# Mixer of a decoder layer: small TensorE steps at counted distances, narrow inverse and state products

## The chip, the cores and the metric

The kernel runs on one core of a Trainium2 chip. The metric is device time in microseconds, the median of several executions. TensorE is PE in the profile, VectorE is DVE, ScalarE is ACT, GpSimd is POOL, and SyncE, which issues most loads, is SP.

## The reference, cut to what matters

One layer of a hybrid decoder, for 256 prompt tokens and one token each of 8 sample sequences. D is 2048, the hidden width 5632, all in float32:

```python
x = x + 0.5 * swiglu(rms_norm(x, g1), w1, w3, w2)          # ffn1
x = x + mixer_block(rms_norm(x, gm), ...)
x = x + mem_attend(rms_norm(x, gq), mem_k, mem_v, w_q, w_o)
x = x + 0.5 * swiglu(rms_norm(x, g2), w1, w3, w2)          # ffn2

# mixer_block
proj = h @ w_in                          # qkv (conv), z, b, a, q_s, k_s, v_s, two gates
# gated delta rule, 8 heads of 128, chunks (the reference takes 64, the kernel 128):
lmat = eye + beta * (k @ k.T) * decay    # lower triangular, unit diagonal
u_v, w_k = solve(lmat, [beta * v, beta * gamma * k])
u = u_v - w_k @ S;  o = q_g @ S + (q @ k.T * decay) @ u;  S = g_end * S + k_end.T @ u
o_g = rms_norm(o) * silu(z)
# sliding window attention, 16 query heads on 4 key heads of 64, window 128, with a sink:
o_s = softmax_with_sink(mask(q_s @ k_s.T / 8)) @ v_s
out = (sigmoid(gate_gdn) * (o_g @ w_br_gdn) + sigmoid(gate_swa) * (o_s @ w_br_swa)) @ w_out
```

The sample rows do one step of the same rule on 8 stored states per head (128x128 each) and attend to a stored cache of 128 keys.

## The kernel before

The activations are kept transposed: 16 chunks of 128 features by 264 columns (256 prompt, 8 sample). Every weight product runs in fp32r with both operands split in a high and a low part. `gemm` (L169) loads a block of weights `raw` (128x1024, L153, from SP's queue, four buffers), ACT casts it to `wh` (L154, three buffers), DVE subtracts to `wl` (L155, four buffers), and PE does three products for each 128x128 tile: `wh` by `xh` (L184), `wh` by `xl` (L185), `wl` by `xh` (L186). A block of four chunks and two column tiles is 24 products of 128x264. These "big products" fill most of every stage: ffn1, the mixer, the memory attention, ffn2.

The mixer's other work is small. `gemm_ba` (L343) makes the decay and beta scalars, with three transposes at L361 to L363. For each of four head pairs `conv_pair` (L435) projects and convolves q, k, v and z, `gdn_pair` (L462) does the prompt's chunked rule for four arrays at once (two heads by two chunks), and `gdn_sample` the eight sample states. The triangular inverse in `gdn_pair` doubles its block size level by level: L536 transposes the first level, then five levels follow, each with four products A by U (L545, 64 columns, into `pP`), a mask on DVE (L547), four products with T (L550, into `pU`), a subtraction on DVE (L551), and transposes of U (L555) with a copy to T on ACT (L556); L560 to L566 close it. The outputs come at L570 to L594, the square, mean and scaling of the output norm at L599 to L609, and its transposes at L612. In `gdn_sample` each of 16 states per pair is the stationary operand of a product with two columns (L653); the states are loaded by SP at the start of that function. Sliding window attention has a projection with rope, then `swa_prompt` for each of four key groups: scores (L770), mask and maximum on DVE (L773 to L779), exponentials on ACT (L780, L782), sum and reciprocal on DVE (L783, L784), scaling on ACT (L786), transposes (L791), a copy (L792), products with the values (L797). One group has three such blocks. `swa_sample` does the same for the sample rows.

In the source the steps stand one after the other, "c0 c1 s c2 w0 c3 w1 x w2 w3", and then 12 of 16 gate products. The order in which each engine really runs them is chosen at build time by a scheduler with a simulated timeline, which takes whichever instruction it expects to be ready: the small steps of one pair end up between big products of later steps. Only in the memory attention are PE's instructions kept in source order (`pin`). PSUM tiles `gd` and `sw` (two buffers each) hold results of small products.

Of the kernel before, what the change touches and what calls it, by code (L numbers as in the profile page):

```python
# [30 lines left out]
    0, 128, 256, 384, 512, 640, 960, 1224, 1488)  # L31
C_N = 1744


def constants():
# [9 lines left out]
    c[:, C_M1:C_M1 + P] = (i % 2 == 1) & (j == i - 1)  # L45
    for n in range(5):
        s = 2 << n
        q = np.arange(64)
        col = (q // s) * 2 * s + s + q % s
        blk = (i // (2 * s) == col[None, :] // (2 * s)) & (i % (2 * s) < s)  # L50
        c[:, C_LV + n * 64:C_LV + (n + 1) * 64] = blk
# [4 lines left out]
    c[:, C_SN:C_SN + TOK] = np.sin(ang) * np.where(np.arange(P) % 64 < 32, -1.0, 1.0)[:, None]  # L56
    k = np.arange(2 * P)[None, :]
# [12 lines left out]
class Build:  # L70
    def __init__(self, ctx, tc, i, o, phases):
        self.tc, self.nc, self.i, self.o = tc, tc.nc, i, o
        nc = self.nc
# [95 lines left out]
    def gemm(self, W, n0, nw, xs, evac, k0=0, steps=()):  # L169
# [18 lines left out]
        for j in range(nt):  # L188
            evac(j, ps[j][:, :TOK])

# [77 lines left out]
    def mixer(self, norm, nxt):  # L268
# [9 lines left out]
        if True:  # L278
            with self.phase("mc") as mc, self.phase("gd", 2, PSUM) as gd, self.phase("sw", 2, PSUM) as sw:
# [21 lines left out]
            for n, g in gates[12:14]:  # L301
                self.gate(win, xs, n, g)
            sp = {"og": self.split_in("og", self.og), "os": self.split_in("os", self.os)}
            for n, g in gates[14:]:
# [38 lines left out]
    def gemm_ba(self, win, xs):  # L343
        nc, mc = self.nc, self.mc
        idn = self.K(C_ID)
        bt = mc.tile([P, 3, 16], F32, name="bt")

# [6 lines left out]
        for c in range(NCH):  # L354
            for k in range(2):
                nc.tensor.matmul(acc, HL[:, c], xs[c][k], start=(c == 0 and k == 0), stop=(c == NCH - 1 and k == 1))
        ba = self.gp.tile([P, TOK], F32, name="cy", bufs=2)[0:32]
        nc.vector.tensor_tensor(out=ba, in0=acc, in1=self.norm.finish()[0:32], op=ALU.mult)
        pt = self.evt()
        i32 = idn[0:32, 0:32]  # L360
        nc.tensor.transpose(pt[:, 0:32], ba[:, 0:P], i32)  # L361
        nc.tensor.transpose(pt[:, 32:64], ba[:, P:NP], i32)
        nc.tensor.transpose(pt[0:NS, 64:96], ba[:, NP:TOK], i32)  # L363
# [22 lines left out]
        nc.vector.scalar_tensor_tensor(out=g, in0=a, scalar=-1.0, in1=b3(ea), op0=ALU.mult, op1=ALU.mult)  # L386
        pg = self.evt()
        nc.tensor.matmul(pg[:, 0:16], self.K(C_UI), g[:, 0:2, :], start=True, stop=True)
        nc.tensor.matmul(pg[:, 16:32], self.ones, g[:, 0:2, :], start=True, stop=True)
# [15 lines left out]
        nc.vector.tensor_tensor(out=dg[:, 1], in0=bc(gs, NS), in1=i8, op=ALU.mult)  # L405
        pb = self.evt()
        nc.tensor.matmul(pb[:, 0:128], self.ones[0:NS, :], dg.rearrange("p a h b -> p (a h b)"), start=True, stop=True)
# [27 lines left out]
    def conv_pair(self, win, xs, p):  # L435
        nc, mc = self.nc, self.mc
        pt = lambda name: mc.tile([P, 2, TOK], F32, name=name, bufs=2)
        self.kp, self.qp, self.vp, self.zp = pt("kp"), pt("qp"), pt("vp"), pt("zp")
        self.conv_group(win, xs, 8 + 2 * p, self.kp)
        self.conv_group(win, xs, 2 * p, self.qp)  # L440
        self.conv_group(win, xs, 16 + 2 * p, self.vp)
        zp = self.zp
# [8 lines left out]
        self.gemm(win, OFF_Z + 2 * p * P, 256, xs, ev)  # L451

# [9 lines left out]
    def gdn_pair(self, p):  # L462
        nc, mc, o = self.nc, self.mc, self.o
        idn = self.K(C_ID)
# [4 lines left out]
        qT = [self.qp[:, hl(a), sl(a)] for a in A4]  # L469
        kT = [self.kp[:, hl(a), sl(a)] for a in A4]  # L470
        vT = [self.vp[:, hl(a), sl(a)] for a in A4]
# [8 lines left out]
        for a in A4:  # L480
            nc.tensor.transpose(pq[:, a], qT[a], idn)
        sq = self.gt("sq")
        nc.scalar.activation(out=sq, in_=pq, func=AF.Square)
        nc.vector.tensor_reduce(out=ss[:, 4:8], in_=sq, axis=AX.X, op=ALU.add)
        pk = self.ps4()
        for a in A4:
            nc.tensor.transpose(pk[:, a], kT[a], idn)
        sq = self.gt("sq")
        nc.scalar.activation(out=sq, in_=pk, func=AF.Square)
        nc.vector.tensor_reduce(out=ss[:, 0:4], in_=sq, axis=AX.X, op=ALU.add)  # L490
        nc.vector.tensor_scalar(out=ss, in0=ss, scalar1=4 * EPS, scalar2=None, op0=ALU.add)
# [7 lines left out]
        ke = self.gt("ke")  # L499
        TT(out=ke, in0=pk, in1=bc(gE, P), op=ALU.mult)  # L500
        kb = self.gt("kb", 2)
        TT(out=kb, in0=pk[:, 1::2], in1=bc(skb[:, 1::2], P), op=ALU.mult)
        pv = self.ps4()
        for a in A4:
# [772 lines left out]
```

## Time and profile before

| | us |
|---|---|
| Median of three runs | 2515.12 (2513.25 to 2518.91) |
| Profiled execution, own time | 2517.21 |
| Its span, first to last instruction | 2515.4 |
| The mixer up to the last small step of its heads | 782 to 1416 of that span |

A timeline row tells when an instruction (or a run of the same ones, "x4") begins and how long it is shown as busy. PE overlaps its instructions, so the rows of two products overlap, and what a product costs is the distance from its start to the next one's. A float32 product has two rows, a float32 transpose and an fp32r product one. "Idle before" tells how long an engine stood still ahead of an instruction, and the name behind the arrow what ended that.

### The profile page before, as it was taken

The page shows a single profiled execution, that of the slowest core. Times are in us where ns is not written, and L with a number is a line of the kernel's source. Part 1 is how long each engine was busy: PE and PEld are TensorE (multiplying, and loading weights), DVE is VectorE, ACT ScalarE, POOL GpSimd, SP SyncE. Part 2 cuts the span into 40 slices and gives each one's busy share as a digit, 9 for nine tenths or more (in the row PEclk, how much of TensorE's full clock was granted, in tenths as well). Part 3 has the DMA queues.
Part 4 walks back from the last instruction along what each step waited for, and adds up shares of the span by engine and source line. Part 5 has one row for each costly group of instructions (what it writes and reads, how often), then busy time and mean ns, then how long its engine had stood idle before and what let it go on. Part 6 is the DMA issues. An engine that isn't in the chain of part 4 may idle for free. (4 is left out here: it accounts for less than half of the span.)

```text
span 2515.4 us, 48048 instructions
## 1 busy us (share of the span) xinstructions
PE 2469.8 (98%) x19960; PEld 2434.6 (97%) x19960; DVE 1508.7 (60%) x2495; ACT 1102.5 (44%) x1631; POOL 109.2 (4%) x159
## 2 busy tenths in 40 slices
PE   7999999999999999999999999999999999999997
PEld 7999999999999998998999999979999999999997
DVE  6555544555556867776575677678555545555554
ACT  5444333444444543454454445445444333444443
POOL 0000000000000002010120410000000000000000
PEclk9999999999999998999999999999999999999999
DMA  6656566656666556454555876765655566565554
GB/s 205 183 178 183 174 181 184 181 180 181 179 178 192 160 154 207 149 160 140 162 160 161 261 220 211 221 235 154 183 182 178 176 183 185 178 183 178 177 172 131
DMA packets 136091, 455.22 MB, mean 181 GB/s; under 512 B 16736, under 2 KB 22976, under 8 KB 135824
## 3 DMA queue, kind: packets, MB, share of 16 engines
q1 hardware_dynamic: 127072, 424.18, 55.6%
q0 software_dynamic: 7504, 24.65, 2.8%
q8 instruction: 156, 2.56, 0.4%
q10 hardware_dynamic: 1296, 3.31, 0.3%
q14 instruction: 63, 0.52, 0.1%
HBM read 438.02 MB, written 14.98 MB: 180 GB/s over the span
## 5 line engine op out<-in xcount | busy, mean ns | idle before, releaser
L155 DVE TENSOR_TENSOR wl<-raw,wh 128x1024 fp32r<-128x1024 f32 (+2 forms) x794 | 953.8, 1202 | 795.1 <-ACT wh L154 789.5
L154 ACT CAST wh<-raw 128x1024 fp32r<-128x1024 f32 (+2 forms) x794 | 817.3, 1030 | 1230.0 <-PE mm L185 630.3
L184 PE MATMUL mm<-xh,wh 128*128 128x264 f32 x2672 | 769.7, 289 | 12.4 <-ACT wh L154 12.4
L185 PE MATMUL mm<-xl,wh 128*128 128x264 f32 x2672 | 770.6, 289 | 0.3 <-DVE xl L1183 0.3
L186 PE MATMUL mm<-xh,wl 128*128 128x264 f32 x2672 | 768.1, 288 | 2.4 <-DVE wl L155 2.4
L184 PEld LDWEIGHTS mm<-xh,wh 128*128 128x128 f32 x2672 | 509.7, 191 | 15.2 <-ACT wh L154 12.6
L186 PEld LDWEIGHTS mm<-xh,wl 128*128 128x128 f32 x2672 | 508.8, 191 | 5.1 <-DVE wl L155 3.2
L185 PEld LDWEIGHTS mm<-xl,wh 128*128 128x128 f32 x2672 | 509.7, 191 | 3.4 <-issue 2.2
L184 PE MATMUL mx<-xh,wh 128*128 128x264 f32 x1424 | 406.6, 286 | 2.1 <-ACT wh L154 2.1
L186 PE MATMUL mx<-xh,wl 128*128 128x264 f32 x1424 | 406.5, 285 | 0.0
L185 PE MATMUL mx<-xl,wh 128*128 128x264 f32 x1424 | 405.6, 285 | 0.0
L184 PEld LDWEIGHTS mx<-xh,wh 128*128 128x128 f32 x1424 | 270.1, 190 | 2.3 <-ACT wh L154 2.3
L185 PEld LDWEIGHTS mx<-xl,wh 128*128 128x128 f32 x1424 | 269.5, 189 | 0.0
L186 PEld LDWEIGHTS mx<-xh,wl 128*128 128x128 f32 x1424 | 269.4, 189 | 0.0
L186 PE MATMUL mm<-hh,wl 128*128 128x264 f32 x748 | 212.8, 286 | 0.0
L184 PE MATMUL mm<-hh,wh 128*128 128x264 f32 x748 | 212.6, 284 | 0.0
L185 PE MATMUL mm<-hl,wh 128*128 128x264 f32 x748 | 212.4, 284 | 0.0
L186 PE MATMUL mx<-hh,wl 128*128 128x264 f32 x660 | 187.7, 285 | 0.0
L184 PE MATMUL mx<-hh,wh 128*128 128x264 f32 x660 | 187.6, 284 | 0.0
L185 PE MATMUL mx<-hl,wh 128*128 128x264 f32 x660 | 187.4, 284 | 0.0
L185 PEld LDWEIGHTS mm<-hl,wh 128*128 128x128 f32 x748 | 140.9, 188 | 0.0
L184 PEld LDWEIGHTS mm<-hh,wh 128*128 128x128 f32 x748 | 140.7, 188 | 0.0
(543 smaller groups left out, 2933.1 us busy)
## 6 DMA issues: line engine op xcount, KB each, us to landing
raw<-in_ffn_w_dram SPq DMA_DIRECT2D x511, 512.0 KB, 3.7
raw<-in_w_in_dram SPq DMA_DIRECT2D x152, 512.0 KB, 3.8
raw<-in_w_out_dram SPq DMA_DIRECT2D x32, 512.0 KB, 3.8
raw<-in_ffn_w_dram SPq DMA_DIRECT2D x33, 256.0 KB, 2.6
raw<-in_w_br_gdn_dram SPq DMA_DIRECT2D x16, 512.0 KB, 4.7
raw<-in_w_br_swa_dram SPq DMA_DIRECT2D x16, 512.0 KB, 4.8
gd<-gt POOLq DMA_DIRECT2D x32, 132.0 KB, 3.4
tg<-gd POOLq DMA_DIRECT2D x32, 132.0 KB, 4.4
```

The lines of the kernel that those rows point to most:

```text
L154: nc.scalar.copy(out=H, in_=raw)
L155: nc.vector.tensor_tensor(out=L, in0=raw, in1=H.bitcast(F32), op=ALU.subtract)
L184: nc.tensor.matmul(acc, wh, xh, start=(kg + c == 0), stop=False)
L185: nc.tensor.matmul(acc, wh, xl, start=False, stop=False)
L186: nc.tensor.matmul(acc, wl, xh, start=False, stop=(kg + c == nk - 1))
```

## The change

All PE instructions go through a helper `te`. While it is on, which is in the mixer only, PE keeps the order of the source. The small work is written as generators; each `yield` ends a step. `tick` is called after every three big products and takes at most one step from the lanes: A (scalars, head pairs, sample states), B (window attention), V (transposes of the value rows). The number behind `yield` is the distance to the lane's next step in ticks of three big products, 6 (18 products) where nothing is named; between any two steps lie at least two ticks. Steps stand in the order "c0 s c1 w0 w1 g2 c2 w2 w3 g2 c3 x g8" (g: gates).

The first four doubling levels of the inverse work on a compact form: only the four 32x32 diagonal blocks of each array are kept, side by side in one 128x128 tile, so that one transpose serves all four arrays and the products have 32 stationary columns, each in its own strip of 32 output partitions, with the moving side expanded by a mask on DVE (`Ue`, `Pe`). The first level's transpose is done on DVE. The fifth level stays as it was. The state products are turned round: `kqz` (32 columns, 8 of them used) is stationary, and four states at a time are moved past it (512 columns); a mask and additions on DVE pick the wanted rows, and one transpose restores the layout. The states are fetched a step before the pair's outputs. In `swa_sample` keys and values are loaded further ahead and the products come in four groups. The scaling of `kb` is an ACT copy and a later DVE product, the transposes of v come later.

```diff
+    def tick(self):
+        self.clock += 1
+        ready = [n for n in self.lanes if n.todo and n.at <= self.clock]
+        if ready and self.clock >= self.last + 2:
+            min(ready, key=lambda n: n.at).step()
+            self.last = self.clock
...
-                    nc.tensor.matmul(acc, wh, xh, start=(kg + c == 0), stop=False)
-                    nc.tensor.matmul(acc, wh, xl, start=False, stop=False)
-                    nc.tensor.matmul(acc, wl, xh, start=False, stop=(kg + c == nk - 1))
+                    self.te.matmul(acc, wh, xh, start=(kg + c == 0), stop=False)
+                    self.te.matmul(acc, wh, xl, start=False, stop=False)
+                    self.te.matmul(acc, wl, xh, start=False, stop=(kg + c == nk - 1))
+                    self.tick()
...
-                self.gemm_ba(win, xs)
                 self.conv_state_load()
-                for step in "c0 c1 s c2 w0 c3 w1 x w2 w3".split():
+                self.te.on = True
+                A, B, V = self.lanes = [Lane(self, 6), Lane(self, 6), Lane(self, 6)]
+                self.lane_v = V
+                A.add(self.gemm_ba(win, xs), 24)
+                for step in "c0 s c1 w0 w1 g2 c2 w2 w3 g2 c3 x g8".split():
                     k = int(step[1:] or 0)
                     if step[0] == "c":
-                        self.conv_pair(win, xs, k)
-                        self.gdn_pair(k)
-                        self.gdn_sample(k)
+                        A.drain(2)
+                        q = self.conv_pair(win, xs, k)
+                        A.add(self.gdn_pair(k, q))
+                        A.add(self.gdn_sample(k, q))
                     elif step[0] == "s":
                         self.swa_proj(win, xs)
                     elif step[0] == "w":
-                        self.swa_prompt(k)
+                        B.add(self.swa_prompt(k))
+                    elif step[0] == "x":
+                        B.add(self.swa_sample())
                     else:
-                        self.swa_sample()
-                for n, g in gates[:12]:
-                    self.gate(win, xs, n, g)
+                        for n, g in gates[:k]:
+                            self.gate(win, xs, n, g)
+                        gates = gates[k:]
+                for n in (A, B, V):
+                    n.drain()
+                self.lanes, self.te.on = [], False
...
+        grp, i32 = self.K(C_GRP, 4), self.K(C_I32, 32)
+        g4 = lambda t: t.rearrange("p (a b) -> p a b", a=4)
+        X, Y = self.gt("sq"), self.gt("d")
+        Ac, t1, tt, Uh = X[:, 0], X[:, 1], X[:, 2], X[:, 3, 0:64]
+        Uc, T2 = Y[:, 0], Y[:, 1]
+        Ue = Y[:, 2:4].rearrange("p a b -> p (a b)").rearrange("p (a b c) -> p a b c", a=4, b=4)
+        for b in range(4):
+            r = slice(32 * b, 32 * b + 32)
+            nc.scalar.copy(out=g4(Ac)[r], in_=A[r, :, r])
+        TT(out=g4(t1), in0=g4(Ac), in1=bm(self.K(C_M1, 32), 4), op=ALU.mult)
+        nc.vector.transpose(out=tt, in_=t1)
+        TT(out=g4(Uc), in0=bm(i32, 4), in1=g4(tt), op=ALU.subtract)
+        for n in range(4):
+            s = 2 << n
+            uh = Uc.rearrange("p (a n two s) -> p (a n) two s", a=4, two=2, s=s)[:, :, 1, :]
+            nc.vector.tensor_copy(out=Uh.rearrange("p (a s) -> p a s", s=s), in_=uh)
+            TT(out=Ue, in0=Uh.rearrange("p (a c) -> p a c", a=4)[:, :, None, :].to_broadcast([P, 4, 4, 16]),
+               in1=grp[:, None, :, None].to_broadcast([P, 4, 4, 16]), op=ALU.mult)
+            yield 10 if n == 0 else None
+            pt = self.gdt()
+            self.te.transpose(pt[:, 0:P], Uc, idn)
+            nc.scalar.copy(out=T2, in_=pt[:, 0:P])
+            pP = self.gdt()
+            for a in A4:
+                self.te.matmul(pP[32 * a:32 * a + 32, 0:64], Ac[:, 32 * a:32 * a + 32], Ue[:, a], start=True, stop=True)
+            Pe = self.gt("Pm", 4, 64).rearrange("p b (a c) -> p b a c", a=4)
+            TT(out=Pe, in0=pP[:, 0:64].rearrange("p (b c) -> p b c", b=4)[:, :, None, :].to_broadcast([P, 4, 4, 16]),
+               in1=self.K(C_LV + n * 64, 64).rearrange("p (a c) -> p a c", a=4)[:, None, :, :].to_broadcast([P, 4, 4, 16]), op=ALU.mult)
+            yield
+            pU = self.gdt()
+            for b in range(4):
+                self.te.matmul(pU[32 * b:32 * b + 32, 0:64], T2[:, 32 * b:32 * b + 32], Pe[:, b], start=True, stop=True)
+            TT(out=uh, in0=uh, in1=pU[:, 0:64].rearrange("p (a s) -> p a s", s=s), op=ALU.subtract)
...
+        Ss = self.state_load(p)
+        tiles.append(Ss)
+        yield
...
+        yield 14
         pt = self.ps4()
         for a in A4:
-            nc.tensor.transpose(pt[:, a], ot[:, a], idn)
...
+        yield 8
+        pX = self.gdt()
+        for m in range(4):
+            self.te.matmul(pX[32 * m:32 * m + 32, :], kqz[:, m], Ss[m].rearrange("p b e -> p (b e)"), start=True, stop=True)
+        xm, own = self.gt("d"), self.gt("sq")[:, 0]
+        TT(out=xm, in0=pX.rearrange("p (b e) -> p b e", b=4), in1=bc(self.K(C_DG, 4), P), op=ALU.mult)
+        TT(out=xm[:, 0:2], in0=xm[:, 0:2], in1=xm[:, 2:4], op=ALU.add)
+        TT(out=own, in0=xm[:, 0], in1=xm[:, 1], op=ALU.add)
+        yield 8
         pk = self.gdt()
-        for h in range(2):
-            for b in range(NS):
-                m = (h * NS + b) * 2
-                nc.tensor.matmul(pk[:, m:m + 2], Ss[h * 2 + b // 4][:, b % 4], kq[:, h, b, :], start=True, stop=True)
-        pks = pk[:, 0:2 * n].rearrange("p (n two) -> p n two", two=2)
...
+            yield 10
             pt = self.swt().rearrange("p (a k q) -> p a k q", a=nh, k=blk + 1)
             for a in range(nh):
                 for kt in kb:
-                    nc.tensor.transpose(pt[:, a, kt], sc[:, a, kt * P:(kt + 1) * P], idn)
+                    self.te.transpose(pt[:, a, kt], sc[:, a, kt * P:(kt + 1) * P], idn)
             nc.scalar.copy(out=pT, in_=pt)
+            yield
...
+class InOrder:
+    def __init__(self, tc):
+        self.tc, self.on = tc, False
+    def matmul(self, *a, **k):
+        ins = self.tc.nc.tensor.matmul(*a, **k)
+        return self.tc.keep_in_program_order(ins) if self.on else ins
+    def transpose(self, *a, **k):
+        ins = self.tc.nc.tensor.transpose(*a, **k)
+        return self.tc.keep_in_program_order(ins) if self.on else ins
+class Lane:
+    def __init__(self, b, gap):
+        self.b, self.gap, self.todo, self.at = b, gap, [], 0
+    def add(self, gen, wait=0):
+        if not self.todo:
+            self.at = max(self.at, self.b.clock + wait)
+        self.todo.append(gen)
+    def step(self):
+        try:
+            n = next(self.todo[0])
+            self.at = self.b.clock + (n or self.gap)
+        except StopIteration:
+            self.todo.pop(0)
+    def drain(self, keep=0):
+        while len(self.todo) > keep:
+            self.step()
```

Three places of PE and ACT show what moved. The first is one level of the inverse on PE, first pair: before, `gd<-idn,U` are the four transposes, `gd<-U,E` the first four products; `mm` rows are big products.

```order
L186 MATMUL mm<-xh,wl 128x264
L555 MATMUL gd<-idn,U 128x128 x4
L545 MATMUL gd<-U,E_9713 128x64 x4
L184 MATMUL mm<-xh,wh 128x264
L185 MATMUL mm<-xl,wh 128x264
```

And after, where `d` holds the compact U:

```order
L1333 MATMUL mm<-xh,wl 128x264
L1337 MATMUL gd<-idn,d 128x128
L1333 MATMUL gd<-d,sq 32x64 x4
L1333 MATMUL mm<-xh,wh 128x264
L1333 MATMUL mm<-xl,wh 128x264
```

Four transposes became one, and four products of 128 stationary columns became four of 32. The second half of a level (L550 before, `gd<-Pm,d 32x64` after) comes 24 products later before and 18 later after.

The second place is PE at the sample states of the first pair, before:

```order
L186 MATMUL mm<-xh,wl 128x264
L653 MATMUL gd<-kq,d 128x2 x4
L653 MATMUL gd<-kq,T 128x2 x4
L653 MATMUL gd<-kq,U 128x2 x4
L653 MATMUL gd<-kq,bv 128x2 x4
L184 MATMUL mm<-xh,wh 128x264
```

and after:

```order
L1333 MATMUL mm<-xh,wl 128x264
L1333 MATMUL gd<-E_10478,w 32x512
L1333 MATMUL gd<-T,w 32x512
L1333 MATMUL gd<-U,w 32x512
L1333 MATMUL gd<-bv,w 32x512
L1333 MATMUL mm<-xh,wh 128x264
```

Sixteen products with the states as weights became four with the states moving.

The third place is ACT at the first block of window attention, before; L782 are the exponentials of the scores, L786 their scaling, L154 casts of weight blocks.

```order
L780 ACTIVATE sm_e<-sm_e 128x4
L154 CAST wh<-raw 128x1024
L782 ACTIVATE sc,sm_s<-sc,sm_m 128x128 x4
L586 COPY u<-gd 128x2x128
L786 ACTIVATE sc<-sc,sm_s 128x128 x4
L154 CAST wh<-raw 128x1024
```

After, the same steps are L883 to L889; `qg` and the two `E` rows are the decay exponentials of the second pair.

```order
L164 CAST wh<-raw 128x1024
L883 ACTIVATE sm_e<-sm_e 128x4
L885 ACTIVATE sc,sm_s<-sc,sm_m 128x128 x4
L544 ACTIVATE qg<-gd 128x256
L547 ACTIVATE E_11636<-E_11636 128x512
L548 ACTIVATE E_11637<-E_11637 128x512
L889 ACTIVATE sc<-sc,sm_s 128x128 x4
L896 COPY pT<-sw 128x512
```

The decay exponentials now stand between the scores' exponentials and their scaling. On PE the products that the decay exponentials read and the transposes that read the scaled scores lie six big products apart:

```order
L1333 MATMUL gd<-c,gg 128x128 x4
L1333 MATMUL mm<-xh,wh 128x264
L1333 MATMUL mm<-xl,wh 128x264
L1333 MATMUL mm<-xh,wl 128x264
L1333 MATMUL mm<-xh,wh 128x264
L1333 MATMUL mm<-xl,wh 128x264
L1333 MATMUL mm<-xh,wl 128x264
L1337 MATMUL sw<-idn,sc 128x128 x4
```

In the program before, the transposes of that block stood behind the pair's output products, with nothing of a decay step near them. The same arrangement comes twice after, in the second and the third pair.

## Rows read from the trace of the kernel before

**Rows 1.** The page: each engine's busy us, share of the span, and instructions.

```profile
PE 2469.8 (98%) x19960; PEld 2434.6 (97%) x19960; DVE 1508.7 (60%) x2495; ACT 1102.5 (44%) x1631; POOL 109.2 (4%) x159
```

**Rows 2.** Windows: stretch, its length, busy us of PE, PEld, DVE, ACT, POOL, clock, DMA share, GB/s.

```profile
50.00:100.00 50.00, 50.00 (x412) 50.00 (x411) 27.24 (x35) 20.40 (x25) 0.00 (x0) 1.00 0.59 180
782.00:1416.00 634.00, 616.39 (x4960) 599.80 (x4960) 440.55 (x1059) 296.16 (x570) 83.82 (x110) 0.98 0.54 169
811.00:815.00 4.00, 3.71 (x19) 3.60 (x20) 4.00 (x19) 1.61 (x6) 0.00 (x0) 0.57 0.32 117
1108.00:1112.00 4.00, 4.00 (x23) 4.00 (x23) 3.01 (x18) 3.67 (x10) 0.00 (x0) 0.57 0.01 3
```

**Rows 3.** PE's waits above 2 us, 782 to 1416 us: sum, times, longest.

```profile
PE ev L361 <- DVE cy L358: 4.0, 1, 4.0
PE sw L791 <- ACT sc L786: 3.5, 1, 3.5
PE gd L511 <- DVE kb L502: 3.4, 2, 2.2
PE gd L653 <- DMA d<-in_state_gdn_dram: 2.6, 1, 2.6
PE mx L184 <- ACT wh L154: 2.1, 1, 2.1
```

**Rows 4.** PE's timeline at one inverse level: start, busy us, line, operands.

```profile
892.35 0.60 PE L555 MATMUL gd<-idn,U 128*128 128x128 f32 x4
892.79 1.00 PE L545 MATMUL gd<-U,E 128*128 128x64 f32 x8
893.60 0.37 PE L184 MATMUL mm<-xh,wh 128*128 128x264 f32 x1
893.81 0.28 PE L185 MATMUL mm<-xl,wh 128*128 128x264 f32 x1
```

**Rows 5.** PE's timeline at the state products of the second pair.

```profile
1104.53 0.95 PE L653 MATMUL gd<-kq,d 128*128 128x2 f32 x8
...
1108.01 0.91 PE L791 MATMUL sw<-idn,sc 128*128 128x128 f32 x4
```

**Rows 6.** PE's timeline at the 32-column products of the memory attention.

```profile
1691.51 0.40 PE L962 MATMUL mm<-wl,osh 128*128 128x512 f32 x1
1691.74 0.40 PE L963 MATMUL mm<-wh,osl 128*128 128x512 f32 x1
1692.07 0.30 PE L1103 MATMUL ap<-xh,mx 128*32 128x128 f32 x2
...
1695.70 2.00 PE L1110 MATMUL ap<-apT,mv 128*128 128x256 f32 x8
```

**Rows 7.** PE's timeline at two pairs of 256-column products of the memory attention.

```profile
1670.67 1.03 PE L1052 MATMUL ap<-KT,cy 128*128 128x256 f32 x4
1671.54 1.03 PE L1052 MATMUL ap<-KT,gt 128*128 128x256 f32 x4
```

**Rows 8.** DVE's, then ACT's timeline from a block's mask to its scaling.

```profile
1071.89 0.76 DVE L773 SCALAR_TENSOR_TENSOR sc<-sw,c 128x256 f32<-128x256 f32 x2
1072.56 1.22 DVE L155 TENSOR_TENSOR wl<-raw,wh 128x1024 fp32r<-128x1024 f32 x1
1073.70 0.68 DVE L775 TENSOR_REDUCE sm_m<-sc 128x4 f32<-128x512 f32 x1
1075.60 1.05 ACT L154 CAST wh<-raw 128x1024 fp32r<-128x1024 f32 x1 [0.38 <-PE mm L185]
1076.56 0.40 ACT L782 ACTIVATE sc<-sc,sm_m 128x128 f32<-128x128 f32 x1
1078.70 1.28 ACT L786 ACTIVATE sc<-sc,sm_s 128x128 f32<-128x128 f32 x4 [0.24 <-DVE sm_s L784]
```

**Rows 9.** ACT and DVE at the same pair's output norm.

```profile
1082.19 0.60 ACT L599 ACTIVATE sq<-gd 128x512 f32<-128x512 f32 x1 [1.28 <-PE gd L591]
1095.66 0.68 DVE L609 TENSOR_TENSOR d<-gd,rn 128x512 f32<-128x512 f32 x1
```

More of the change, by code (lines that the diff above doesn't have):

```diff
@@ L72, in __init__ @@
         self.tc, self.nc, self.i, self.o = tc, tc.nc, i, o
+        self.te = InOrder(tc)
+        self.clock, self.last, self.lanes = 0, 0, []
         nc = self.nc
@@ L498, in gdn_pair @@
         TT(out=skb, in0=sA, in1=gam, op=ALU.mult)
[L499 to L504, printed above, removed]
-            nc.tensor.transpose(pv[:, a], vT[a], idn)
-        bv = self.gt("bv")
-        TT(out=bv, in0=pv, in1=bc(sbv, P), op=ALU.mult)
+        TT(out=kb, in0=kb, in1=bc(skb[:, 1::2], P), op=ALU.mult)
+        yield
         pG = self.ps4()
@@ new lines, in gdn_pair @@
+        T, U = self.gt("T"), self.gt("U")
+        nc.vector.transpose(out=tt, in_=Uc)
+        full = lambda t: t.rearrange("p a (b c) -> p a b c", b=4)
+        gb = grp[:, None, :, None].to_broadcast([P, 4, 4, 32])
+        TT(out=full(U), in0=g4(Uc)[:, :, None, :].to_broadcast([P, 4, 4, 32]), in1=gb, op=ALU.mult)
+        TT(out=full(T), in0=g4(tt)[:, :, None, :].to_broadcast([P, 4, 4, 32]), in1=gb, op=ALU.mult)
+        uh = [U[:, a].rearrange("p (n two s) -> p n two s", two=2, s=32)[:, :, 1, :] for a in A4]
@@ new lines, in gdn_pair @@
+        uall = U.rearrange("p a (n two s) -> p (a n) two s", two=2, s=32)[:, :, 1, :]
+        yield 8
+        pP = self.ps4(4, 64)
+        for a in A4:
+            self.te.matmul(pP[:, a], A[:, a], uh[a], start=True, stop=True)
+        Pm = self.gt("Pm", 4, 64)
+        TT(out=Pm, in0=pP, in1=bm(self.K(C_LV + 256, 64), 4), op=ALU.mult)
+        yield
+        pU = self.ps4(4, 64)
+        for a in A4:
+            self.te.matmul(pU[:, a], T[:, a], Pm[:, a], start=True, stop=True)
+        TT(out=uall, in0=uall, in1=pU.rearrange("p a (n s) -> p (a n) s", s=32), op=ALU.subtract)
@@ L557, in gdn_pair @@
+        yield
+        pT = self.ps4()
+        for a in A4:
+            self.te.transpose(pT[0:64, a, 0:64], U[0:64, a, 0:64], idn[0:64, 0:64])
+        nc.scalar.copy(out=T[0:64, :, 0:64], in_=pT[0:64, :, 0:64])
         lo, up = slice(0, 64), slice(64, P)
@@ L674, in gdn_sample @@
         pn = self.gdt()
-        nc.tensor.matmul(pn[:, 0:n], self.ones, t, start=True, stop=True)
+        self.te.matmul(pn[:, 0:n], self.ones, t, start=True, stop=True)
         so, rn = st("sso"), st("srn")
@@ L817, in swa_sample, with keys @@
                 nc.vector.tensor_copy(out=knT[half(q), t, :], in_=self.kd[2 * t + q][half(q), sc])
-        ps = self.swt()
-        for b2 in range(0, NS, 2):
+        def keys(b2):
             kc = self.kc_tile()
@@ L823, in swa_sample, with values @@
             nc.vector.tensor_copy(out=kT[:, :, :, 0].rearrange("p b t -> p t b"), in_=knT[:, :, b2:b2 + 2])
-            for b in (b2, b2 + 1):
-                for t in range(2):
-                    nc.tensor.matmul(ps[:, b * 16 + t * 8:b * 16 + t * 8 + 8], kT[:, b - b2, t], qb[:, b, t], start=True, stop=True)
+            return kT
+        def values(b2):
+            vc = self.kc_tile()
+            nc.sync.dma_start(out=vc, in_=i["cache_v"][:, b2:b2 + 2])
+            nc.gpsimd.dma_start(out=vc[0:1], in_=self.vn[b2:b2 + 2, :])
+            return vc
+        kTs, vcs = [keys(b2) for b2 in (0, 2, 4)], []
+        yield 24
+        ps = self.swt()
+        for n in range(4):
+            if n:
+                yield
+            for b in (2 * n, 2 * n + 1):
+                for t in range(2):
+                    self.te.matmul(ps[:, b * 16 + t * 8:b * 16 + t * 8 + 8], kTs[n][:, b % 2, t], qb[:, b, t], start=True, stop=True)
+            if n == 0:
+                kTs.append(keys(6))
+            else:
+                vcs.append(values(2 * n - 2))
         sp2 = mc.tile([P, 2, P], F32, name="kcT", bufs=2)
@@ L848, in swa_sample @@
         po = self.swt()
[L849 to L853 removed]
+        for k in range(4):
+            yield 16 if k == 3 else None
+            for b in (2 * k, 2 * k + 1):
                 for t in range(2):
                     n = b * 16 + t * 8
[L856 removed]
+                    self.te.matmul(po[:, n:n + 8], vcs[k][:, b % 2, t * P:(t + 1) * P], pT[:, n:n + 8], start=True, stop=True)
+            if k == 0:
+                vcs.append(values(6))
         for par in range(2):
```

276 lines of the change are left out of this document (149 added, 127 removed).

## The prediction

> **What bounds the kernel now.** I read the page's busy shares first, then the windows by stretch, PE's waits inside the mixer, and the timeline at the places the change touches. PE is busy 98% of the span; no other engine is above 60% [rows 1]. So a change is worth what it takes out of PE's row or puts into it. The windows show what a full PE looks like: 412 big products (128x264) in 50 us, one every 121.4 ns, granted clock 1.00 [rows 2]. The mixer up to its last small step, 782 to 1416 us, is where the edits lie. It is 634 us long at a clock of 0.98. At 121.4 ns its 3,703 big products (the split products L184 to L186 and the 32 of L356, counted in the trace) come to 449.5 us; the remaining 184.5 us are what can be argued about: small steps, waits, half clock, and the slower first product after a small step.
>
> The waits of that stretch add up to 17.7 us, 15.6 of them in five causes [rows 3] and the rest in late weight blocks. Half clock shows as short spells: 811 to 815 us has a clock of 0.57 and 19 products where the first window's pace gives 33, and 0.57 from 1108 to 1112 as well [rows 2]. That is the lower of the two clock levels for most of the stretch. The first came behind a wait, 4.0 us for the first transposes [rows 3]. The second came with no wait: it follows sixteen state products that PE ran without a pause [rows 5].
>
> **The change part by part.**
>
> *Small products that go.* The row of one inverse level [rows 4]: four transposes start at 892.35, the four L545 products at 892.79, the next big product at 893.60. So four transposes take 0.44 us of PE and four 128x64 products 0.81. Per head pair the change removes four full transposes-by-four of the levels and the four of the first level (5 x 0.44 = 2.2), and the L545 and L550 groups of four levels (8 x 0.81 = 6.5). The fifth level stays wide. State products: sixteen of two columns run from 1104.53 to 1108.01, 3.48 us [rows 5]. Four pairs: 4 x (2.2 + 6.5 + 3.5) = 48.7 us.
>
> *Small products that come.* Per level one transpose (0.44 / 4 = 0.11) and two groups of four 32-column products with 64 columns moving; per pair one state group of four 32-column products with 512 columns moving, and one transpose. Nothing in the mixer before is shaped so, but the memory attention's L1103 is: 32 output columns, four strips. 64 products (128 rows) run from 1692.07 to 1695.70, 0.227 us for each four, with 128 columns moving [rows 6]. That is 0.057 a product, where a wide product of half the columns costs 0.20 [rows 4], so strips run beside each other. Low bound for a group with 64 columns: half of that, 0.11; high bound: no overlap, 0.81 as L545. I take 0.227, since it is the row of the same kind. 32 groups: 7.3 us (3.6 to 25.9). State group: two 128x256 float32 products take 0.87 us [rows 7], so a 512-column one takes 0.87 alone; four beside each other 0.87, four in turn 3.48. I take 0.87: 3.5 us (to 13.9). With 20 transposes of 0.11 (2.2) the sum is 13.0 us, bounds 9.3 and 42.
>
> Net: **-35.7 us** of PE time, bounds -39 and -7.
>
> The Trainium skill, page "TensorEngine Tiling (Array Packing)", section "Tiling Modes", speaks against this: changing the tiling mode drains TensorE. The row bears it out in size: the first L1103 starts 0.33 us after the last L963, where L963 itself starts 0.23 after its neighbour [rows 6]. By the rule 36 groups would each pay about 0.1 us more, some 3.6 us as an estimate, and the net would be -32.
>
> *Other engines.* DVE gains compaction, masks and expansions (2,027 rows before, 2,069 after in the program's order), ACT is level. DVE stands at 440.6 us busy in 634 [rows 2]. I cost this at nothing by load; what matters is what stands in front of a needed result in DVE's and ACT's order, the next part.
>
> *Order and distance: the waits.* Before, PE's order was arranged by a scheduler that put a small step where its operands were expected; 24 products (2.9 us) lay between two hops of the inverse, 75 to 99 between the output norm and its transposes. After, PE takes the steps at counted places, most 18 products (2.19 us) apart, and a step that is late stops every product behind it. I walked the after order with durations from the trace:
> - Softmax of the window attention, 12 blocks. Scores to transposes are now 30 to 36 products, some 4.0 us, with up to 1.3 us of other small steps. Before, the chain took 7.8 us: DVE begins at 1071.89, a subtraction of 1.22 us comes between, the maximum is at 1073.70, a cast of 1.05 at 1075.60, the exps start at 1076.56, the scaling at 1078.70 [rows 8]; the transposes themselves came much later. Taking out the idle stretches leaves about 5.0 us (an estimate from these rows) plus whatever cast or subtraction lies inside. In the second and third pair it is worst: ACT's order puts the three decay exps of the pair (one of 256, two of 512 columns; a 512-column pass is 0.60 [rows 9]) and DVE's order three 512-column steps between exps and scaling, while PE stands only 6 products (0.73 us) behind the cumulative-decay products that these wait for. From there to the first scaled score I count 3.9 us, so a wait of about 3.3 twice. The other ten blocks come out 1 to 2 us short, taken as 1.3: 6.6 + 13 = 20 us in all.
> - Output norm, 4 pairs: 42 products (5.1 us) for square, reduce, reciprocal root and scaling. Before, from 1082.19 to the scaling at 1095.66 [rows 9], which was in no hurry; the bare chain with a subtraction and a cast inside is about 7.4. Short by 2.3: 9 us.
> - First hops: the first transposes still wait for the evacuation (4.0 in rows 3; only its neighbours moved): 4 us. The first pair's first level, where rope work is in DVE's queue: 4. Others (decay products, rope's distance): 3.
> - The L184 wait of 2.1 at the stretch's end is untouched: 2.
> - The other inverse hops: need 1.9 to 2.1 against 2.19, taken as 0.
>
> Sum after 42 us, before 17.7: **+24 us**. What goes is the wait of L653 for its DMA (2.6), as the states are now fetched a step earlier into tiles that are free, and that of L511 for L502 (3.4), as the scaling moved off the path; late next are the scores. Bounds: 10 us after, if casts seldom stand in between, and 78, if they often do (the second rival works it out). A wait that is added stops the big products queued behind it on PE, and with them the release of weight buffers; SP and POOL only get earlier loads.
>
> *Half clock.* Eight spells in and at the end of the stretch cost some 15 us in all: products at 0.22 instead of 0.12 us over 3.4 us each, one of 10.2, as the rows of PE's timeline were counted. Those behind state products should go; but waits of 2 us and longer, five before [rows 3] and each with a spell behind it, become about nine. Nine short ones at 1.5 us are 14: taken as **0**, bounds -10 and +10.
>
> *Number of places.* 158 groups of small steps before and 160 after, so the slow first product behind a group (0.21 instead of 0.12 [rows 4]) stays: 0.
>
> **Sum.** -35.7 + 24 + 0 = -12 us on the profiled execution's own 2517.2 (2 more than its span), which is 2505; the median of the timed runs is 2515.1, 2 lower, so **2503**.
>
> **Rivals.**
> 1. *The distances suffice.* If ACT and DVE deliver within the counted products (before, hops of 24 products left no wait in the inverse: none is named [rows 3]), after has some 10 us of waits and four or five spells: -35.7 - 8 - 8 = about -52, or 2463 us. For: DVE is idle 30% and ACT more than half of the stretch [rows 2]. Against: the walk above, and the scores' 30 to 36 products. Chance 0.22.
> 2. *Slower: PE fixed, everybody else late.* The place is the inverse and output hops of the four pairs, some 80. A hop needs 1.9 to 2.1 us of its 2.19; with a cast of 1.05 or a subtraction of 1.22 [rows 8] in front it is about 0.9 late. A block of weights lasts PE 24 products, 2.91 us, and brings one of each, so every second hop may meet one: 80 x 0.45 = 36 us beside the 42, 78 in all, and -35.7 + (78 - 17.7) = +25, or 2540 us. It decides from waits of 53 us in the stretch (17.7 + 35.7). For: the order has no way round a late step, and ACT ran the exps of a block only when a cast was through [rows 8]. Against: blocks are cast ahead (three buffers, four for the low parts), so a late hop leaves the next casts early, out of the way. Chance 0.24.
> 3. *The narrow products don't run beside each other.* Then the saving is 7 and waits +24: +17, 2532 us. For: 64 moving columns are short against the loading of 32-column weights, which no row shows at that size. Against: L1103's 0.057 us a product [rows 6]. Chance 0.05.
>
> My forecast has the remaining 0.49.
>
> **How the numbers follow.** 0.2% of the time, about what a measurement of this kernel can tell from no change, is 5 us: faster ends at 2510.1, slower begins at 2520.1. The forecast's own spread (waits 25 to 50, saving 37 to 32) is -30 to 0, 2485 to 2515: faster 0.36, same 0.12, slower 0.01 of its 0.49. Rival 1 is faster throughout (0.22). Rival 2 reaches into "same" a little (0.02) and is slower in 0.22; rival 3 slower (0.05). Together: faster 0.58, same 0.14, slower 0.28. The range takes in most of rival 1 and most of rival 2: 2460 to 2534; the forecast's own, 2485 to 2515, stands beside it.
>
> **What would show it.** Right: four narrow rows within 0.3 us and a state group under 1.2 us; PE's row about 36 us less in the mixer apart from waits and clock; waits of PE in the stretch near 42 us, led by the transposes of scores behind ACT's scaling (two over 3 us) and of outputs behind the scaling of the norm; none at L653's successor for a DMA; no half clock right behind state products. Wrong: waits under 20 (rival 1), or a wait at most inverse hops, for the expansion on DVE or the copy on ACT (rival 2); narrow groups of 0.6 us and more (rival 3).

## The result, and the profile after

The changed kernel took 2549.55 us (median of four runs, 2548.95 to 2555.39) against 2514.18 for the kernel before: ratio 1.0142, interval 1.0122 to 1.0162. The forecast was 2503. Its profiled execution took 2549.74 us with a span of 2547.9.

The page's first lines, in answer to [rows 1]: PE is busy 21.5 us less, and the span is 32.5 us longer.

```profile
span 2547.9 us, 47864 instructions
PE 2448.3 (96%) x19804; PEld 2396.2 (94%) x19804; DVE 1521.5 (60%) x2555; ACT 1103.0 (43%) x1651; POOL 109.0 (4%) x159
```

PE's waits from 782 to 1450 us, in answer to [rows 3] (sum, times, longest):

```profile
PE sw L1337 <- ACT sc L889: 13.9, 8, 2.9
PE gd L1337 <- DVE d L684: 9.5, 4, 2.6
PE sw L1337 <- DVE grt L156: 9.3, 1, 9.3
PE gd L1333 <- DVE ke L526: 6.8, 1, 6.8
PE gd L1337 <- DVE d L579: 5.9, 1, 5.9
PE mm L1333 <- DVE sq L385: 5.5, 1, 5.5
PE mm L1333 <- DVE cX L449: 3.4, 1, 3.4
PE gd L1337 <- DVE su L755: 3.3, 2, 1.7
PE sw L1337 <- DVE gry L157: 3.0, 1, 3.0
PE ev L1333 <- issue: 2.8, 1, 2.8
...
PE gd L1333 <- DVE d L584: 2.6, 1, 2.6
```

With the smaller ones these are 72.2 us, where before had 17.6. The two largest single waits, 9.3 and 6.8 us, come just after the third and the fourth pair begin (at 1147.5 and 1284.9 us).

The windows, in answer to [rows 2]: the granted clock of the whole stretch is 0.94 where it was 0.98, and 0.73 in the 12 us around the longest wait, in which PE works 2.66.

```profile
782.00:1450.00 668.00, 595.63 (x4792) 561.90 (x4792) 453.34 (x1119) 296.04 (x588) 83.86 (x110) 0.94 0.50 161
1146.00:1158.00 12.00, 2.66 (x18) 2.12 (x18) 7.04 (x26) 4.63 (x16) 7.06 (x9) 0.73 0.63 218
```

The narrow products themselves, on PE's timeline; first one group of an inverse level (answers [rows 4]), then the state products of the third pair (answers [rows 5]):

```profile
889.13 0.28 PE L1333 MATMUL mm<-xh,wl 128*128 128x264 f32 x1
889.34 0.32 PE L1333 MATMUL gd<-Pm,d 128*32 128x64 f32 x8
889.59 0.39 PE L1333 MATMUL mm<-xh,wh 128*128 128x264 f32 x1
889.82 0.28 PE L1333 MATMUL mm<-xl,wh 128*128 128x264 f32 x1
...
1255.19 0.28 PE L1333 MATMUL mm<-xh,wl 128*128 128x264 f32 x1
1255.40 0.62 PE L1333 MATMUL gd<-E,w 128*32 128x512 f32 x1
...
1256.40 0.39 PE L1333 MATMUL mm<-xh,wh 128*128 128x264 f32 x1
```

Four narrow products take 0.25 us (0.81 before), the state group 1.00 (3.48 before). The product in front of each group is followed after 0.21 us instead of 0.12.

To put all kernels side by side I summed PE's timeline, of the one profiled execution of each, from 780 us until the same 4,059 big products had run; in every kernel all small steps lie inside. A big product counts 0.1214 us (492.8 in all); "half clock" is what big products cost above that where the granted clock is at the lower of its two levels, "edges" what they cost above it otherwise (mostly the first product behind a small step and the last ahead of one), "small" the distance that small steps take.

| us | small | waits | half clock | edges | sum | median of runs |
|---|---|---|---|---|---|---|
| before | 133.1 | 17.6 | 12.4 | 18.9 | 674.8 | 2514.18 |
| after | 96.3 | 72.2 | 21.4 | 26.3 | 709.0 | 2549.55 |
| difference | -36.8 | +54.6 | +9.0 | +7.4 | +34.2 | +35.4 |

So the saving came as reckoned and was paid back one and a half times over in waits, with half clock and edges on top.

What the largest wait is shows only when the engines are laid side by side. DVE, POOL, ACT and PE at the start of the third pair:

```profile
1144.00 1.18 DVE L880 TENSOR_TENSOR sm_m<-sm_m,small 128x4 f32<-128x4 f32 x1
...
1147.91 0.68 DVE L542 TENSOR_TENSOR d<-gd,sc 128x512 f32<-128x512 f32 x1
1153.31 0.69 DVE L526 TENSOR_TENSOR ke<-gd,sc 128x512 f32<-128x512 f32 x1 [4.72 <-POOL U L784]
...
1154.52 0.68 DVE L545 SCALAR_TENSOR_TENSOR E<-d,c 128x512 f32<-128x512 f32 x1
...
1156.13 0.16 DVE L887 RECIPROCAL sm_s<-sm_s 128x4 f32<-128x4 f32 x1
...
1143.86 1.30 POOL L784 TENSOR_TENSOR E<-E,ke 128x512 f32<-128x512 f32 x1
...
1151.02 1.04 POOL L780 TENSOR_TENSOR u<-u,w 128x512 f32<-128x512 f32 x1 [1.58 <-DMA u<-ud]
1152.02 1.26 POOL L784 TENSOR_TENSOR U<-U,ke 128x512 f32<-128x512 f32 x1
...
1148.63 0.38 ACT L544 ACTIVATE qg<-gd 128x256 f32<-128x256 f32 x1 [0.31 <-DVE d L542]
1155.28 0.63 ACT L547 ACTIVATE E<-E 128x512 f32<-128x512 f32 x1 [6.27 <-DVE E L545]
...
1156.39 1.28 ACT L889 ACTIVATE sc<-sc,sm_s 128x128 f32<-128x128 f32 x4
...
1147.22 0.28 PE L1333 MATMUL mm<-xh,wl 128*128 128x264 f32 x1
1156.85 1.35 PE L1337 MATMUL sw<-idn,sc 128*128 128x128 f32 x4 [9.34 <-DVE grt L156]
```

DVE's next instruction at 1148.6 writes tile `ke`. The sample step of the pair before uses the same tile for its state update, whose last use on POOL starts at 1152.02; 1.58 us of the delay is POOL's own wait for the load of `u`, a step in front of it. DVE stands 4.72 us with all that is queued behind it; the decay exponentials on ACT wait for DVE (L545), the scaling of the scores (L889) is queued behind the exponentials, and PE waits for the scaling. The scaling also needs the reciprocal (L887), which stands in DVE's queue as well and is through at 1156.29, so by these rows the exponentials in front cost it only 0.1 us more. The name in PE's row, L156, is merely the event that came last: no transpose of scores reads it. At the fourth pair DVE stands 4.9 us at L545, which writes E1, for the store of the state that sat in that tile:

```profile
1286.34 0.88 DVE L545 SCALAR_TENSOR_TENSOR E<-d,c 128x512 f32<-128x512 f32 x1 [4.94 <-DMA out_gdn_s_dram<-E]
```

### The profile page after: what moved, and what is told of

Read it like the earlier page. It is cut to its first block, busy times and chain, and to the rows that moved or that the text cites. A ratio compares the mean times of both kernels' runs of the same rounds, so it can differ in the third digit from the quotient of the medians.

```text
span 2547.9 us, 47864 instructions
## 1 busy us (share of the span) xinstructions
PE 2448.3 (96%) x19804; PEld 2396.2 (94%) x19804; DVE 1521.5 (60%) x2555; ACT 1103.0 (43%) x1651; POOL 109.0 (4%) x159
## 4 chain that ended last, share of the span: by engine, by line
PE 90%; DVE 4%; DMA 2%; ACT 2%; issue 1%; SPq 0%; POOL 0%; ACTq 0%; DVEq 0%; POOLq 0%
PE mm L1333 53%; PE mx L1333 32%; PE gd L1333 2%; DVE wl L165 1%; DMA raw<-in_w_in_dram 1%; ACT wh L164 1%; PE sw L1333 1%; PE ap L1333 1%; PE sw L1337 0%; PE gd L1337 0%; DMA cth<-cy 0%; DMA x<-in_x_dram 0%; DMA out_gdn_s_dram<-E 0%; SPq L801 0%; PE fps L1337 0%
## 5 line engine op out<-in xcount | busy, mean ns | idle before, releaser
L165 DVE TENSOR_TENSOR wl<-raw,wh 128x1024 fp32r<-128x1024 f32 (+2 forms) x794 | 960.3, 1210 | 814.2 <-ACT wh L164 808.7
L1333 PE MATMUL mm<-xh,wh 128*128 128x264 f32 (+1 forms) x2688 | 790.5, 294 | 20.4 <-ACT wh L164 11.5
L1333 PE MATMUL mm<-xl,wh 128*128 128x264 f32 (+1 forms) x2688 | 772.9, 288 | 0.7 <-DVE xl L1309 0.7
L1333 PEld LDWEIGHTS mm<-xh,wh 128*128 128x128 f32 (+1 forms) x2688 | 516.6, 192 | 34.0 <-issue 14.3
L1333 PEld LDWEIGHTS mm<-xl,wh 128*128 128x128 f32 (+1 forms) x2688 | 515.9, 192 | 1.2 <-DVE xl L1309 0.9
```

The source lines that it names most:

```text
L165: nc.vector.tensor_tensor(out=L, in0=raw, in1=H.bitcast(F32), op=ALU.subtract)
L1333: ins = self.tc.nc.tensor.matmul(*a, **k)
```

## The experiments

Lines of all tables are made as above. Each was timed against the kernel before on the same chip (its medians there 2511.5 to 2514.1). The smaller edits of the change (states fetched earlier and the first of them into E1, where before it was `d`; the scaling of `kb`; the transposes of v; the loads of `swa_sample`) stay in all of them and are not priced apart.

**e1: the narrow products alone**, under the scheduler, in the source order of before.

```diff
-                self.te.on = True
+                self.te.on = False
...
-                for step in "c0 s c1 w0 w1 g2 c2 w2 w3 g2 c3 x g8".split():
+                A.drain()
+                for step in "c0 c1 s c2 w0 c3 w1 x w2 w3 g12".split():
...
```

Lanes are drained at once after each step, so no tick places anything.

> Narrow inverse and state products alone: source order and scheduler of the kernel before, no fixed order on PE. Theory A (the narrow products save PE time as reckoned, the fixed order costs it in waits): small steps of the mixer 37 us less than before, waits near the 18 of before, so about 2480 us. Rival B (the longer chain through DVE that the narrow form needs is what makes PE wait): waits well above 18, and a time near or above 2514.

**e2: the fixed order alone**, with the inverse, state products and constants of the kernel before, cut into steps in the same way (one step more at the first level, one fewer at the sample states).

```diff
-        for n in range(4):
+        for n in range(5):
...
-                self.te.matmul(pP[32 * a:32 * a + 32, 0:64], Ac[:, 32 * a:32 * a + 32], Ue[:, a], start=True, stop=True)
+                self.te.matmul(pP[:, a], A[:, a], uh[a], start=True, stop=True)
...
```

> The fixed order and its distances alone, with the wide inverse and state products of the kernel before. Theory A: the waits of the changed kernel (72 us) and its half clock stay, the 37 us of small steps come back: about 2585 us. Rival B (the waits come from the narrow form's DVE chain): waits fall to some 40 us, so about 2550. Both keep the two waits of 9.3 and 6.8 us at the start of the third and fourth pair if these come from tile reuse.

| us | small | waits | half clock | edges | sum | median | ratio to before, interval |
|---|---|---|---|---|---|---|---|
| e1 | 98.0 | 23.1 | 11.5 | 24.2 | 649.5 | 2491.08 | 0.9906 (0.9888 to 0.9923) |
| e2 | 129.8 | 51.3 | 17.2 | 23.2 | 714.1 | 2556.81 | 1.0169 (1.0147 to 1.0192) |

The narrow products save 35 us of small steps; waits and edges take back 5 each, so that the sum is 25 us less, and the medians are 20 apart on that chip (the profiled execution of before ran 3 us above its median). Theory A holds, 11 us short of its 2480. The fixed order alone costs 45 us. Its time lies near B's 2550 and not at A's 2585: the wide form waits 51 us, not 72. So under a fixed order B has a part: the first level of the first pair waits 8.5 us in the narrow form and 1.3 here, the sample steps 5.6 and nothing, the output norm 9.5 and 6.3, the scores apart from the longest wait 16.9 and 14.8. The two long waits are there in both forms, so they belong to the order:

```profile
PE sw L1299 <- DVE gry L151: 12.6, 2, 9.6
PE gd L1295 <- DVE ke L520: 7.9, 1, 7.9
```

Under the scheduler the tiles are reused too: in e1 DVE stands once, 2.6 us, at the write of E1 for a store, and the longest wait of PE near it is 4.3 us.

**e3 and e4: the reused tiles.** e3 puts 40 ticks behind each sample step; e4 takes tile `u` for all four pieces of the state update.

```diff
                 nc.gpsimd.dma_start(out=o["gdn_s"][2 * p + h, :, hb * 4:hb * 4 + 4], in_=S)
+        yield 40
...
-                ub = self.gt(("ke", "u")[hb])
+                ub = self.gt("u")
```

> The changed kernel with 40 ticks (120 big products, 14.6 us) more between the end of one pair's sample step and the start of the next pair. Theory R (the waits of 9.3 and 6.8 us come from tiles ke and E1 that POOL's state update and the store of a state still hold, which stops DVE's queue for 4.7 and 4.9 us): no DVE idle stretch there, these two waits fall from 16 to 4 us or less, the half clock behind them goes too, about 2533 us. Rival W (the decay exponentials in front of the score's scaling, as walked by hand, make them): the wait of 9.3 falls only if the two no longer meet; others stay, 2545 us.

> The changed kernel with one edit: the four pieces of the state update all use tile u, so that ke is free when the next pair begins; E1 is still a state tile. Theory R: the DVE stop of 4.7 us behind POOL at the third pair is gone and its wait of 9.3 us falls to about 3 (the decay exponentials stay in front); at the fourth pair the stop behind the store of E1 stays (some 5 to 7 us); about 2540 us. Rival W: the wait of 9.3 stays above 6, 2548 us.

| us | small | waits | half clock | edges | sum | median | ratio, interval |
|---|---|---|---|---|---|---|---|
| e3 | 96.0 | 66.0 | 25.7 | 25.0 | 705.4 | 2549.04 | 1.0132 (1.0108 to 1.0156) |
| e4 | 95.8 | 67.2 | 25.0 | 25.5 | 706.2 | 2547.75 | 1.0134 (1.0114 to 1.0153) |

DVE's stops moved as theory R says, and neither time did; the times are rival W's (2545 and 2548). In e3 the wait of 6.8 is gone and that of 9.3 is 5.4, but the other five score transposes of that stretch wait 15.0 us instead of 7.1:

```profile
PE sw L1338 <- ACT sc L890: 20.4, 6, 5.4
```

Shifted by 14.6 us, lane A's steps meet lane B's elsewhere; at the wait of 5.4 DVE's softmax steps run beside POOL's update and take 1.19 and 1.01 us (L882, L887) instead of 0.16. That this is the reason is argued, not shown. In e4 DVE no longer stands at `ke`, and stands 3.1 us at the next instruction of the same sort, the write of E1:

```profile
1144.50 0.15 DVE L886 TENSOR_TENSOR sm_s<-sm_s,sm_e 128x4 f32<-128x4 f32 x1
1147.79 0.95 DVE L545 SCALAR_TENSOR_TENSOR E<-d,c 128x512 f32<-128x512 f32 x1 [3.14 <-DMA out_gdn_s_dram<-E]
```

PE's wait there is 6.7 us, not theory R's 3, which is W's sign. But e4 is no clean test: with one tile `u` the four pieces of the update stand some 7 us apart on POOL, the last store goes out later, and DVE stands 2.4 and 7.0 us at a new place, the write of `bv`. So neither run lowers the time: while the distances were short, another late step took the place of the one that was removed.

**e5, e6, e9, e10: longer distances**, e5 with these edits, e6 with the 40 ticks of e3 as well, e9 with 20 ticks, e10 with 30 and three more distances.

```diff
-            yield 10 if n == 0 else None
+            yield (30 if p == 0 else 14) if n == 0 else None
...
-        yield 14
+        yield 24
...
-            yield 10
+            yield 20
```

The second is the output norm, the third the scores; two in the sample step go from 8 to 12 and from 10 to 18. e10 against e6:

```diff
-            yield (30 if p == 0 else 14) if n == 0 else None
+            yield (46 if p == 0 else 14) if n == 0 else None
...
-        yield 24
+        yield 36 if p == 0 else 24
...
-        yield 40
+        yield 30
...
-            yield 16 if k == 3 else None
+            yield 26 if k == 3 else None
```

> The changed kernel with longer distances at the places that waited: scores to transposes 20 ticks for 10, output norm 24 for 14, first inverse level 30 (first pair) and 14 for 10, state products 12 for 8 and 18 for 10; nothing else. Theory D (distances too short for chains that run through two queues in order): waits of the window attention (17), the norm (9.5), the first level (8.4) and the sample steps (5.6) go to a few us, those of the start (8) and of the reused tiles (up to 16) stay, so some 30 us of waits instead of 72 and half as much half clock: about 2500 us. Rival M (a fixed order only moves waits, as with 40 ticks between pairs, where two went and others grew by nearly as much): waits above 55, time above 2535.

> As the run with longer distances, and 40 ticks between a sample step and the next pair, so that the state update's tiles are free. Theory D with R: waits about 15 us (start 8, end, a little), half clock near that of before, about 2480 us, under the narrow products with the scheduler (2491). Rival M: waits above 40, over 2515 us.

> Long distances and 20 ticks (7.3 us) instead of 40 between a sample step and the next pair: half the dose. Theory R (the next pair's first writes wait for POOL's state update and a store, which end some 15 us after the last sample step): a part of the two waits of 11.9 and 7.8 us stays, 4 to 10 us in all, 2487 to 2495 us. Rival (any gap will do, it is the meeting of lanes): 2482.

> Long distances with four more changes where the best run still waited: first level of the first pair 46 ticks for 30, its output norm 36 for 24, last group of sample values 26 for 16, and 30 ticks between pairs for 40. Theory D: waits of 3.9, 3.0 and 2.5 us go, half clock behind the first and third too; about 2472 us. Rival (chains held by DMA of rope and values, not by distance): 2480.

| us | small | waits | half clock | edges | sum | median | ratio, interval |
|---|---|---|---|---|---|---|---|
| e5 | 93.1 | 44.1 | 13.7 | 22.8 | 666.5 | 2508.23 | 0.9980 (0.9970 to 0.9990) |
| e6 | 90.0 | 26.1 | 7.2 | 23.7 | 639.8 | 2481.92 | 0.9872 (0.9849 to 0.9894) |
| e9 | 90.1 | 25.1 | 10.1 | 23.6 | 641.8 | 2483.72 | 0.9884 (0.9867 to 0.9900) |
| e10 | 89.3 | 20.5 | 7.4 | 24.6 | 634.7 | 2474.78 | 0.9847 (0.9832 to 0.9861) |

Theory D's 2500 and 30 us of waits for e5 came out as 2508 and 44; rival M's 2535 is out. e5's PE waits: the eight of the scores have become one, and the two behind the reused tiles are now the largest.

```profile
PE gd L1333 <- DVE E L555: 11.9, 1, 11.9
PE gd L1333 <- DVE ke L526: 7.8, 1, 7.8
PE mm L1333 <- DVE sq L385: 5.5, 1, 5.5
PE gd L1337 <- DVE d L684: 5.5, 2, 2.8
PE gd L1333 <- DVE d L584: 3.9, 1, 3.9
PE sw L1337 <- ACT sc L889: 3.2, 1, 3.2
```

Not all of these two is DVE standing still for a tile. It stands 3.7 us in front of the first (the row names a POOL addition; the store of the state in E1 lands at 1138.36) and 1.1 in front of the second. Beside POOL's instructions, moreover, six of DVE's steps from 1127 to 1140 us take 5.1 us more than the same steps elsewhere in this trace (L165 1.22, L151 0.16, L545 0.68):

```profile
1128.10 2.30 DVE L165 TENSOR_TENSOR wl<-raw,wh 128x1024 fp32r<-128x1024 f32 x1
1130.33 1.24 DVE L151 TENSOR_SCALAR gry<-ss 128x8 int32<-128x8 int32 x1
...
1138.45 1.76 DVE L545 SCALAR_TENSOR_TENSOR E<-d,c 128x512 f32<-128x512 f32 x1 [3.67 <-POOL U L784]
```

With the gap both waits are gone, and 26 us of time with them (e6 against e5): 18.0 us of waits, 6.5 of half clock. The gap takes away the stops and the steps beside POOL together, so how much of it is the tiles' stays open. What 40 ticks did not buy alone they buy here. e6 has the expected time (2480), with waits of 26 where 15 were expected. e9's time is the rival's (2482), not theory R's 2487 to 2495: with 20 ticks `ke` costs PE 0.4 us and the decay step 1.4, where I had 4 to 10. Its trace does not contradict R, since DVE's stops were only 3.7 and 1.1 us here and 20 ticks are 7.3. No run gave the update tiles of its own, which would tell the two apart. e10 brings the first pair's waits of 3.9 and 3.0 and the values' 2.5 to nothing, and is the fastest kernel here, 1.5% under before. At its 30 ticks DVE still stands 1.3 and 3.2 us at `ke`; the waits of PE that follow are 2.2 (scores) and 1.6 (L555). Its waits that are left:

```profile
PE sw L1338 <- ACT sc L890: 6.6, 3, 3.2
PE mm L1334 <- DVE sq L385: 5.5, 1, 5.5
PE ev L1334 <- issue: 2.8, 1, 2.8
PE mm L1334 <- DVE wl L165: 1.8, 2, 1.3
PE gd L1338 <- DVE E L555: 1.6, 1, 1.6
```

**e8: the order alone at distances that suffice**, the wide form with e6's distances.

> Fixed order with the long distances and the 40 ticks between pairs, and the wide inverse and state products of the kernel before: order alone, at distances that suffice. Theory D: waits about as in the narrow one (26 us), small steps 33 us longer, so about 2515 us: a fixed order gains nothing by itself, the narrow products are the gain. Rival O (the order itself saves): 2500 us or less.

| us | small | waits | half clock | edges | sum | median | ratio, interval |
|---|---|---|---|---|---|---|---|
| e8 | 125.1 | 21.7 | 17.1 | 22.1 | 678.6 | 2519.98 | 1.0025 (1.0012 to 1.0039) |

As theory D: a fixed order by itself gains nothing, even well spaced (+6 us). The narrow products are worth 38 us on top of it (e6), 20 on top of the scheduler (e1); between the two lie half clock (10 us less from e8 to e6, 1 from before to e1) and edges (1.6 more against 5.3); the waits grow about equally (4.4 and 5.5).

**e7: POOL's part on DVE**, e6 with the update's products and additions issued by `nc.vector` instead of `nc.gpsimd`.

> As the run before, with POOL's eight products and additions of the state update per pair on DVE instead. Theory P (DVE steps of 4 to 16 elements that take 0.5 to 1.2 us beside a POOL product or addition are slowed by it, and so are the chains): such steps back at 0.15 us, waits some 5 us less, but 32 steps of 0.68 us more on DVE: within 5 us of the run before. Rival N (POOL is no cause): the extra 22 us of DVE work add waits, over 10 us slower.

2492.67 us, ratio 0.9917 (0.9894 to 0.9941), 10.75 slower than e6; waits 30.2 (those of the scores 8.3 instead of 3.2), half clock 12.9. The number is rival N's, but its reason is not shown: DVE's small steps no longer stretch to a microsecond anywhere in the mixer, while DVE now stands itself for the update's loads, for instance:

```profile
1123.87 0.69 DVE L780 TENSOR_TENSOR ke<-ke,w 128x512 f32<-128x512 f32 x1 [2.32 <-DMA ke<-ud]
1132.37 0.69 DVE L780 TENSOR_TENSOR ke<-ke,w 128x512 f32<-128x512 f32 x1 [2.74 <-DMA ke<-ud]
```

What the two engines' contention costs PE stays open.

## Why the prediction was wrong

- *Small products: right.* -36.8 us against -35.7. Narrow group 0.25 (0.227), state group 1.00 (0.87). Rival 3 is out.
- *Number of places at 0: wrong by 7.* Entering a 32-column group costs 0.09 us more (0.21 against 0.12), 36 times 3.2 us; 20 of the groups stand behind a big product and so 1.8 us of it in edges, the others stand behind a transpose. The sentence drawn from the Trainium skill, page "TensorEngine Tiling (Array Packing)", section "Tiling Modes", a drain at each change of mode, had 3.6 us as its estimate; the trace agrees, and I had left it out of the sum. The rest of the edges is not the narrow groups': e2, which has none, has 4.3 us more than before as well.
- *The step that failed is "Sum after 42 us".* Measured 72.2: 30 of the 47 us by which the forecast missed (half clock 9, edges 7). The parts that I had walked came near it: scores apart from the 9.3 16.9 (20 with two of 3.3), output norm 9.5 (9), end 2.0 (2). Twice too small were the start, 8.3 for 4, and the first pair's first level, 8.5 for 4. Wholly missed were the reused tiles: "the states are now fetched a step earlier into tiles that are free" asked whether the tile was free for the load and not who waits for it afterwards. E1 is written by the next pair's third step, and `ke`, whose product moved ahead in the pair, by its second; together 9.3 and 6.8 us, of which the walk had 3.3 and DVE's two stops are 4.7 and 4.9. Not walked either were DVE's steps beside POOL's update: at the fourth pair L151 takes 1.23 us instead of 0.17 and L549 1.48 instead of 0.41. And what I took at 3 was 11: the sample steps 5.6, a convolution (L449) 3.4, behind rope steps on DVE that took 1.1 to 1.5 us beside POOL and 0.42 elsewhere, the fifth inverse level 1.1, and small ones. From after to e5 28 us of waits go with the distances, and 19.7 us, the two at the pairs' starts, with the gap (e6, e9). That DVE stopped at the reused tiles is shown; how the 19.7 divide between these stops and the steps beside POOL is not.
- *Half clock at 0: wrong by 9.* I counted nine spells of 1.5 us; the trace's clock has 14 in this stretch, 21.4 us together, where before had eight with 12.4 (not the 15 that I took). Their number is what costs: the spell at the longest wait lasts 10.2 us, but PE stands for most of it and loses 1.3. None stands right behind a state group, as forecast. With the long waits gone e6 has five spells and 7.2 us, below before.
- *Rival 2* came nearest (2540, with 78 us of waits) and had its point of decision (53 us) right, but by luck, since its place is wrong: apart from the first pair's first level one hop of the inverse waits above 0.2 us (1.1, L635). Elsewhere 18 products suffice there, as the forecast said.
- *Rival 1* is what e6 and e10 are, once the distances are right: 2482 and 2475, not 2463, since some 20 us of waits have other causes (the start, 8.3, is in all fixed orders).

## What to carry to other kernels

When the order of one engine is fixed, count the chain through the other engines in their own order, and look at every tile a moved step writes: who read it last, on which engine, and what is queued behind the write. Shorten work and fix an order in separate steps; here one was worth 20 us and the other cost 45, and only longer distances and a gap between the pairs, both together, made the two worth more than the first alone. A wait removed alone proves little while a second late step stands behind it.

## What the runs showed of the hardware

A DVE step of four elements with two inputs took 1.18 us (L880 at 1144.00) beside a POOL addition that ran from 1143.86 to 1145.16; it ended at 1145.18, just behind the addition. The same step takes 0.16 in e7, where POOL has no such work. The Trainium skill, page "SBUF — State Buffer", section "SBUF: two separate sides", says that the two engines share a pair of ports which one of them holds for a whole instruction when a DVE step has two inputs in SBUF; the trace agrees. The change did not bring such stretching: over the mixer it comes to some 25 us of DVE's time before and 20 after (an estimate: each step above the shortest of its line and shape, where that is over 0.25 us).
